# A two-layer hybrid encoder: the order of all five engines drawn on another machine model, and two dependent paths traced at the highest priority

## The chip, the cores and the metric

One Trainium2 chip, of which this program uses one core. The core has five engines that each run their own instruction stream in a fixed order: TensorE (PE, matmuls, with its weight loads shown apart as PEld), VectorE (DVE), ScalarE (ACT), GpSimd (POOL) and SyncE (SP, which here only issues DMAs). The metric is the device time of one launch in microseconds (us); lower is better.

## The reference

A sequence of 512 tokens with 1,024 channels in float32 passes two layers. Each layer normalises, projects once, runs four head groups side by side and projects back:

```python
for i in range(DEPTH):                                   # 2
    h = _rms_norm(x, pre_norm_w[i])                      # x: (1, 512, 1024)
    proj = jnp.einsum("bld,de->ble", h, w_in[i])
    (m_z, m_xbc, m_dt, r_u, r_g, d_q, d_k, d_v, d_g, g_q, g_k, g_v, g_g) = _split(proj, PROJ_SIZES)
    y_a = _mamba_mixer(m_z, m_xbc, m_dt, ...)            # conv, SSD scan in both directions, gated norm
    y_b = _rwkv_mixer(r_u, ...) * jax.nn.silu(r_g)       # delta-rule scan, 8 heads of 64, both directions
    y_c = _diff_mixer(d_q, d_k, d_v, ...) * jax.nn.silu(d_g)   # two softmax maps per head
    y_d = _gqa_mixer(g_q, g_k, g_v, ...) * jax.nn.silu(g_g)    # grouped-query attention
    mix = jnp.einsum("ble,ed->bld", jnp.concatenate([y_a, y_b, y_c, y_d], axis=-1), w_out[i])
    x = x + _rms_norm(mix, post_norm_w[i])
```

The two scans are recurrences. `_wkv7_scan` updates a 64x64 state per head and token with S = S*w + (S a) b + v k; `_ssd` does a scan in chunks of 128 tokens, in 2 groups of 4 heads, forwards and backwards. Everything else (the projections, the attention, the output product `mix`) has no order of its own beyond its inputs.

## The kernel before

**Matmuls and weights.** Products of the projections are made in three matmuls, high part by high part, high by low, low by high. A weight block of 128x512 comes in by a DMA of 256 KB that SP issues (`wf`), ACT makes its high part (`whi`, L144) and POOL its low part (`wlo`, L145), and PE uses the block in 24 matmuls of 256 columns (`pjt`, token-major) or 12 of 512 (`pjc`, channel-major). All of `mm` is L82.

**A layer.** After the first norm, `rwkv` runs: `prep(0)` prepares the first pair of heads, `products(0, 0)` makes the first `pa`, and then a loop over j in 0..3 (a pair of heads in both directions) has the solver and the chain. The solver is one dependent path: a transpose, 15 steps of substitution of two small DVE operations each (L560, L562), two transposes (L567, L568) into `DN` and `DT`, then products on PE, each copied out by ACT and DVE before the next: `pm`, three `ph`, `px`, `pu`, `pq`, `pw`, `pp`, `py`. The chain has 7 steps of `bk` on PE and one DVE operation (L663) each, and `yb`. In its last steps it also makes the next `pa` (`products(j + 1, 0)`), masked on DVE at L450, from which the next solver starts.

Beside the solver's steps the program traces two other kinds of work. `ahead` holds the preparation of the next pair, the transposes to tokens (`pb` among them) and the norm of the last pair. `fill` holds the filler: the projections of the two attentions (`pjt`), their scores `sc`, the transposed probabilities `ptp` and their products `ob`. The `F_` constants say how much filler, in modelled us, is traced after each step.

Then `ssd` runs: the path of the step size (`pjd`, `pcx`), `project(0)` (`pjc`, `pjt`, `pxt`, `pg`), and for each group g of two the same body: for 4 heads two `prow`, the differences on DVE (L811), exponentials on ACT (L814), scaling on DVE (L819, L820), `mt` (L823) and `yd`; then three steps of states (`stp`), four of outputs (`po`), and a norm. The filler beside group 0 is `project(1)`; beside group 1 it is `accumulate`, the output product `mix` with its transposes `ytr` (L1228) and its split of the weights and of y (L1234, L1241, L1242). The rest of `mix` follows the loop and ends the layer.

**What sets the order.** The tile framework takes the instructions in the order of tracing as their priority, gives them to a scheduler that plays them on a modelled machine, and writes each engine's stream in the order in which the model issued them. The streams are then fixed: on the chip an engine waits for the next instruction of its stream, whatever else may be ready behind it. So the place at which filler is traced is a wish, and the model decides.

Of the kernel before, what the change touches and what calls it, by code (L numbers as in the profile page):

```python
# [2 lines left out]

# [1 line left out]

# [26 lines left out]
F_S1 = 0.54  # L32
F_S2 = 0.67
F_S3 = 0.92
F_S4 = 1.0
# [40 lines left out]
def trunk(ctx: ExitStack, tc: tile.TileContext, x_in, win, wwd, wdt, wout, w2a, cols, rows, sscal, consts, out, dbg=None,  # L76
# [38 lines left out]

    x_dram = dpool.tile([L, D], F32, name="x_dram")
    y_dram = [dpool.tile([128, L], F32, name=f"y_dram{n}") for n in range(12)]

    def tap(name, ap, dst=None):
        if dbg is not None and name in dbg:  # L120
# [132 lines left out]
    def rwkv(i, lay, pw, ps, rp, fill):  # L253
# [271 lines left out]
        for j in range(4):  # L525
# [7 lines left out]
                ahead.gens.append(prep(j + 1))  # L533

            def step(n, us):
                ahead(n)
                fill(us)


            sv = rp.tile([128, 1536], F32, tag="sv", name="sv", bufs=1)  # L540
            As = sv[:, 0:1024].rearrange("p (t h s) -> p t h s", t=16, h=2)
# [108 lines left out]
            St = [Q[:, d, 0, :] for d in range(2)]  # L650
            for cc in range(1, 8):
                if cc == C_LAG:
                    ahead.finish()
                    if j < 3:
                        ahead.gens = [products(j + 1, 0)]
                Sn = [None, None]
                for d in range(2):
                    if cc < 7:
                        bk = ps.tile([128, 8, 64], F32, tag="g" if d else "ch", name=f"bk{d}")
                        for e in range(2):  # L660
                            mm(bk[half[e], 0, :], P[half[e], d, cc, :], St[d][half[e]], True, True)
                        Sn[d] = rp.tile([128, 64], F32, tag=f"S{d}", name=f"S{d}", bufs=2)
                        V.scalar_tensor_tensor(Sn[d], bk[:, 0, :], lamC[:, d, cc:cc + 1], Q[:, d, cc, :],  # L663
                                               op0=ALU.mult, op1=ALU.add)
                    for e in range(2):
                        mm(yb[half[e], rev(d, cc)], St[d][half[e]], R[half[e], d, cc, ::1 - 2 * d], False, True, True)
                St = Sn
                step(2, F_CH)
            ahead.finish()
            ys = rp.tile([128, L], F32, tag="tmp", name="ys", bufs=3)  # L670
            for b in range(2):
                sl = lambda t: t.rearrange("p (c b t) -> p c b t", c=4, b=2)[:, :, b, :]
                V.tensor_tensor(sl(ys), sl(yb), Y0[:, b], op=ALU.add)
        for _ in norm(3, ys):
            fill(F_GN / 4)
        fill.scale = 1.0
# [2 lines left out]
    def ssd(i, lay, ps, sp, op, yA, fill, more):  # L679
# [10 lines left out]
        for h, tag in enumerate(("whi", "wlo")):  # L690
# [2 lines left out]
            G.tensor_tensor(w[:, :, 1, :], wf[:, h], w.bitcast(F32)[:, :, 0, :], op=ALU.subtract)  # L693
            ws.append(w.rearrange("p k a n -> p k (a n)"))
        fill.settle()
        pd = ps.tile([128, L], F32, tag="pj", name="pjd")
        for k in range(8):
            mm(pd, ws[k // 4][:, k % 4, :], hT["hi"][:, k, :], k == 0, False)
# [39 lines left out]
            S.activation(colT[:, n], pcx, AF.Copy)  # L738
        exT = sp.tile([128, 4, 64], F32, tag="exT", name="exT")
        S.activation(exT, colT[:, 0], AF.Exp)  # L740

        gr = [{}, {}]

# [47 lines left out]
        for g in range(2):  # L791
            if g:
                fill.finish()
                fill.gens.extend(more)
            cv, zs, xs, bt, gT = (gr[g][n] for n in ("cv", "zs", "xs", "bt", "gT"))

            etot = sp.tile([128, 2, 4, 4], F32, tag="etot", name="etot")
# [2 lines left out]
            for h in range(4):  # L800
                ex = []
                for d in range(2):
                    ri = d * 8 + 4 * g + h
                    pr = ps.tile([128, L], F32, tag="g", name="prow")
                    mm(pr, selE[:, ri:ri + 1].to_broadcast([128, 128]), acs, True, True)
                    p4 = pr.rearrange("p (c t) -> p c t", c=4)
                    S.activation(etot[:, d, :, h:h + 1], p4[:, :, 127:128] if d == 0 else p4[:, :, 0:1], AF.Exp)
                    ar = sp.tile([128, 4, 128], F32, tag="ar", name="ar", bufs=2)
                    row = 32 * d + 4 * g + h
                    for ch in range(4):  # L810
                        V.scalar_tensor_tensor(ar[:, ch, :], p4[:, ch, :], colT[:, 0, ch, row:row + 1],  # L811
                                               mneg[:, d * 128:d * 128 + 128],
                                               op0=ALU.subtract, op1=ALU.min)
                    S.activation(ar, ar, AF.Exp)  # L814
                    ex.append(ar)
                    fill(F_S1)
                for ch in range(4):
                    row = 4 * g + h
                    V.tensor_scalar(ex[0][:, ch, :], ex[0][:, ch, :], colT[:, 1, ch, row:row + 1], None, op0=ALU.mult)  # L819
                    V.scalar_tensor_tensor(ex[1][:, ch, :], ex[1][:, ch, :], colT[:, 1, ch, row + 32:row + 33],  # L820
                                           ex[0][:, ch, :], op0=ALU.mult, op1=ALU.add)
                mt = sp.tile([128, 4, 128], F32, tag="mt", name="mt", bufs=2)
                V.tensor_tensor(mt, ex[1], gT, op=ALU.mult)  # L823
                fill(F_S2)
                if h % 2 == 0:
                    yd = ps.tile([128, 4, 2, 64], F32, tag="g", name="yd")
                for ch in range(4):
                    mm(yd[:, ch, h % 2, :], mt[:, ch, :], xs[:, ch, h * 64:h * 64 + 64], True, True)
                if h % 2 == 1:
                    S.activation(y[:, :, (h - 1) * 64:(h + 1) * 64], yd.rearrange("p c h v -> p c (h v)"), AF.Copy)  # L830

            H = [[None] * 4, [None] * 4]
            for step in range(3):
                stp = ps.tile([128, 2, 256], F32, tag="g", name="stp")
                for d in range(2):
                    ch = step if d == 0 else 3 - step
                    nx = ch + 1 if d == 0 else ch - 1
                    row = 32 * d + 4 * g
                    xd = sp.tile([128, 4, 64], F32, tag="xd", name="xd", bufs=2)
                    G.tensor_tensor(xd, xs[:, ch, :].rearrange("p (h v) -> p h v", h=4),  # L840
                                    colT[:, 2, ch, row:row + 4].unsqueeze(2).to_broadcast([128, 4, 64]), op=ALU.mult)
                    mm(stp[:, d, :], bt[:, ch, :], xd.rearrange("p h v -> p (h v)"), True, True)
                    hn = sp.tile([128, 256], F32, tag=f"H{d}{step}", name="H")
                    if step == 0:
                        V.tensor_copy(hn, stp[:, d, :])
                    else:
                        G.tensor_tensor(hn.rearrange("p (h v) -> p h v", h=4),
                                        H[d][ch].rearrange("p (h v) -> p h v", h=4),
                                        etot[:, d, ch, :].unsqueeze(2).to_broadcast([128, 4, 64]), op=ALU.mult)
                        V.tensor_tensor(hn, hn, stp[:, d, :], op=ALU.add)  # L850
                    H[d][nx] = hn
                fill(F_S3)
            for ch in range(4):
                po = ps.tile([128, 2, 256], F32, tag="g", name="po")
                ds = [d for d in range(2) if H[d][ch] is not None]
                for d in ds:
                    mm(po[:, d, :], cv[6 + g][:, ch * 128:ch * 128 + 128], H[d][ch], True, True)
                of = sp.tile([128, 2, 256], F32, tag="of", name="of", bufs=2)
                for d in ds:
                    row = 32 * d + 4 * g  # L860
                    V.tensor_tensor(of[:, d, :].rearrange("p (h v) -> p h v", h=4),
                                    po[:, d, :].rearrange("p (h v) -> p h v", h=4),
                                    exT[:, ch, row:row + 4].unsqueeze(2).to_broadcast([128, 4, 64]), op=ALU.mult)
                    G.tensor_tensor(y[:, ch, :], y[:, ch, :], of[:, d, :], op=ALU.add)
                fill(F_S4)
                sk = sp.tile([128, 256], F32, tag="sk", name="sk", bufs=2)
                G.tensor_tensor(sk.rearrange("p (h v) -> p h v", h=4), xs[:, ch, :].rearrange("p (h v) -> p h v", h=4),
                                rws[:, R_D + 4 * g:R_D + 4 * g + 4].unsqueeze(2).to_broadcast([128, 4, 64]), op=ALU.mult)
                V.scalar_tensor_tensor(y[:, ch, :], sk, 0.5, y[:, ch, :], op0=ALU.mult, op1=ALU.add)
# [5 lines left out]
                jk = sp.tile([128, 256], F32, tag="sk", name="jk", bufs=2)  # L875
                S.activation(jk, y[:, ch, :], AF.Square, accum_out=ss[:, ch:ch + 1])
            r = rstd(sp, ss, 4, 1.0 / 256, EPS)
            fill(F_S5)
            yA[g] = zs
            for ch in range(4):  # L880
                V.scalar_tensor_tensor(yA[g][:, ch, :], y[:, ch, :], r[:, ch:ch + 1],  # L881
                                       rws[:, R_SSM + g * 256:R_SSM + g * 256 + 256], op0=ALU.mult, op1=ALU.mult)
            tap("ya", yA[g], lambda a: a[:, g * 256:g * 256 + 256].rearrange("(c p) v -> p c v", p=128))


    def softmax_rows(sc, ap):
# [565 lines left out]
```

## Time and profile before

| | us |
|---|---|
| runs | 1826.45, 1837.58, 1839.16 (median 1837.58) |
| the profiled execution | 1827.76, of which the span is 1826.0 |
| granted TensorE clock, mean of the span | 0.93 |
| PE busy | 1596.3, 87% of the span |
| DVE busy | 1088.5, 60% |
| ACT busy | 826.5, 45% |
| POOL busy | 695.9, 38% |

The page gives the busy time of each engine over the span, which for PE says how long some matmul was in flight and not how fast it went. The granted clock says which share of full speed the chip allowed to TensorE. The stretches below are cut at events of the program in layer 1: the first `pm` of each j (143.5, 294, 452.5, 591 us), the end of the last chain (676), the first `prow` of the SSD's group 0 (734) and the end of its last `po` and start of group 1 (about 795), the last `po` of group 1 (839) and the end of `mix` (901). Layer 2 repeats them from about 943 us on.

### The profile page before, as it was taken

The numbers are of one execution on the slowest core, as the hardware profiler recorded it, in microseconds if no ns is written. First come the engines' busy times: TensorE is split into PE (matmuls) and PEld (weight loads), VectorE is DVE, ScalarE is ACT, GpSimd is POOL, SyncE is SP. The second block draws the span as 40 slices with busy tenths as digits, with TensorE's granted clock in tenths as the row PEclk, the third lists the DMA queues.
The fourth block names the chain that finished last, engine by engine and source line by source line (L and its number), as shares of the span: only waits on it lengthen the run. The fifth ranks groups of instructions, "written<-read, shape, count | busy, mean of one in ns | idle before, by whom it ended". The sixth has DMA issues, their size and how long they took to land. (4 is left out here: it accounts for less than half of the span.)

```text
span 1826.0 us, 36868 instructions
## 1 busy us (share of the span) xinstructions
PE 1596.3 (87%) x15232; PEld 1321.8 (72%) x15232; DVE 1088.5 (60%) x2130; ACT 826.5 (45%) x1602; POOL 695.9 (38%) x708
## 2 busy tenths in 40 slices
PE   6888889879899898988887998898788989989888
PEld 6677767757788776766775787677567777768666
DVE  3577576575555437885245865755755554288852
ACT  4645336417345335543346453454272453454431
POOL 4543234242424234543455422343333332245333
PEclk9889989989999998999998899899898999989899
DMA  4110001011101014122321100111110110131223
GB/s 148 64 50 32 29 33 59 14 67 35 42 19 62 28 53 138 59 94 81 127 99 54 53 20 29 34 59 36 44 42 31 36 58 22 54 130 53 87 86 116
DMA packets 57512, 108.50 MB, mean 59 GB/s; under 512 B 6784, under 2 KB 8704, under 8 KB 57344
## 3 DMA queue, kind: packets, MB, share of 16 engines
q1 hardware_dynamic: 57344, 106.15, 17.4%
q8 instruction: 119, 1.95, 0.4%
q14 instruction: 49, 0.40, 0.1%
HBM read 95.64 MB, written 10.49 MB: 58 GB/s over the span
## 5 line engine op out<-in xcount | busy, mean ns | idle before, releaser
L145 POOL TENSOR_TENSOR wlo<-wf,whi 128x512 fp32r<-128x512 f32 x228 | 319.6, 1408 | 423.8 <-ACT whi L144 391.3
L82 PE MATMUL pjt<-whi,hhi 128*128 128x256 f32 x960 | 291.3, 303 | 3.7 <-ACT raw L270 1.7
L82 PE MATMUL pjt<-wlo,hhi 128*128 128x256 f32 x960 | 284.5, 297 | 0.8 <-POOL wlo L145 0.8
L82 PE MATMUL pjt<-whi,hlo 128*128 128x256 f32 x960 | 285.2, 297 | 0.0
L144 ACT ACTIVATE whi<-wf 128x512 fp32r<-128x512 f32 x228 | 142.1, 627 | 226.3 <-PE pjt L82 122.6
L82 PEld LDWEIGHTS pjt<-whi,hhi 128*128 128x128 f32 x960 | 191.8, 200 | 15.6 <-issue 7.3
L82 PEld LDWEIGHTS pjt<-whi,hlo 128*128 128x128 f32 x960 | 191.9, 200 | 6.1 <-issue 5.0
L82 PEld LDWEIGHTS pjt<-wlo,hhi 128*128 128x128 f32 x960 | 191.2, 199 | 5.2 <-issue 3.3
L82 PE MATMUL pjc<-hhi,whi 128*128 128x512 f32 x384 | 160.0, 417 | 16.9 <-ACT craw L751 10.7
L82 PE MATMUL pjc<-hhi,wlo 128*128 128x512 f32 x384 | 157.4, 410 | 3.5 <-POOL wlo L145 3.5
L82 PE MATMUL pjc<-hlo,whi 128*128 128x512 f32 x384 | 156.5, 407 | 0.0
L82 PE MATMUL mix<-whi,ylo 128*128 128x512 f32 x256 | 105.8, 413 | 5.5 <-DVE ylo L1234 5.5
L892 ACT ACTIVATE p<-sc,nm 128x512 f32<-128x512 f32 x96 | 65.6, 685 | 89.0 <-DVE nm L889 81.8
L82 PE MATMUL mix<-wlo,yhi 128*128 128x512 f32 x256 | 103.7, 405 | 0.0
L82 PEld LDWEIGHTS pjc<-hhi,whi 128*128 128x128 f32 x384 | 75.0, 195 | 39.5 <-ACT craw L751 12.4
L82 PE MATMUL mix<-whi,yhi 128*128 128x512 f32 x256 | 99.8, 412 | 4.0 <-ACT yhi L1233 4.0
L889 DVE TENSOR_REDUCE nm<-sc 128x1 f32<-128x512 f32 x96 | 64.5, 689 | 63.2 <-PE sc L82 63.1
L82 PE MATMUL pa<-AR,BK 64*64 64x128 f32 x1024 | 66.3, 341 | 37.7 <-DVE AT L450 37.5
L82 PEld LDWEIGHTS pjc<-hhi,wlo 128*128 128x128 f32 x384 | 75.2, 196 | 23.3 <-POOL wlo L145 5.6
L82 PE MATMUL sc<-qT,qT 64*128 64x512 f32 (+1 forms) x256 | 86.4, 478 | 3.8 <-ACT y L1050 1.8
L82 PEld LDWEIGHTS pa<-AR,BK 64*64 64x64 f32 x1024 | 52.8, 171 | 48.7 <-DVE AT L450 42.4
L82 PEld LDWEIGHTS pjc<-hlo,whi 128*128 128x128 f32 x384 | 75.6, 197 | 15.0 <-issue 0.7
(360 smaller groups left out, 3645.4 us busy)
## 6 DMA issues: line engine op xcount, KB each, us to landing
wf<-in_win_dram SPq DMA_DIRECT2D x224, 256.0 KB, 3.0
wf<-in_wout_dram SPq DMA_DIRECT2D x64, 256.0 KB, 2.7
y<-y_dram SPq DMA_DIRECT2D x24, 256.0 KB, 3.4
xt<-in_x_dram SPq DMA_DIRECT2D x8, 512.0 KB, 4.2
y_dram<-y SPq DMA_DIRECT2D x16, 256.0 KB, 3.3
y_dram<-rs SPq DMA_DIRECT2D x8, 256.0 KB, 2.8
x_dram<-t SPq DMA_DIRECT2D x8, 256.0 KB, 2.1
xt<-x_dram SPq DMA_DIRECT2D x4, 512.0 KB, 4.0
```

The costliest lines, as they stand in the source:

```text
L82: PE.matmul(o, lhsT, rhs, start=start, stop=stop, skip_group_check=skip)
L144: S.activation(hi, wf, AF.Copy)
L145: G.tensor_tensor(lo, wf, hi.bitcast(F32), op=ALU.subtract)
L889: V.tensor_reduce(nm, sc, axis=AX, op=ALU.max, negate=True)
L892: S.activation(p, sc, AF.Exp, bias=nm, accum_out=sm)
```

## The change

The tile context gets `schedule_with_timeline_sim=True`: the order is drawn by playing the instructions on another model of the machine, the timeline machine, with the same priorities as far as the program gives them. And two paths are traced inside `tc.high_priority()`, which puts them ahead of everything else that is ready: the RWKV's solver and chain of each j, and the SSD's step-size path and its body per group. The calls of `ahead` and `fill` within are wrapped in `usual()`, which leaves the high priority for their length. `prep(0)`, `project`, the attention and `accumulate` stay at the usual priority. The instructions and their number are the same; their lines move down by 9 to 23.

```diff
+    urgent = ExitStack()
+
+    @contextmanager
+    def usual():
+
+        urgent.close()
+        yield
+        urgent.enter_context(tc.high_priority())
...
             def step(n, us):
-                ahead(n)
-                fill(us)
-
+                with usual():
+                    ahead(n)
+                    fill(us)
+
+            urgent.enter_context(tc.high_priority())
...
                 if cc == C_LAG:
-                    ahead.finish()
+                    with usual():
+                        ahead.finish()
                     if j < 3:
                         ahead.gens = [products(j + 1, 0)]
...
                 V.tensor_tensor(sl(ys), sl(yb), Y0[:, b], op=ALU.add)
+            urgent.close()
...
         fill.settle()
+        urgent.enter_context(tc.high_priority())
         pd = ps.tile([128, L], F32, tag="pj", name="pjd")
...
         S.activation(exT, colT[:, 0], AF.Exp)
+        urgent.close()
...
             if g:
                 fill.finish()
                 fill.gens.extend(more)
+            urgent.enter_context(tc.high_priority())
...
                     ex.append(ar)
-                    fill(F_S1)
+                    with usual():
+                        fill(F_S1)
...
             tap("ya", yA[g], lambda a: a[:, g * 256:g * 256 + 256].rearrange("(c p) v -> p c v", p=128))
+            urgent.close()
...
-    with tile.TileContext(nc) as tc:
+    with tile.TileContext(nc, schedule_with_timeline_sim=True) as tc:
```

The calls `fill(F_S2)` to `fill(F_S5)` are wrapped in the same way as `fill(F_S1)`.

**PE's stream in layer 1, at the first `pa` of the first pair of heads, before:**

```order
L82 MATMUL pa<-AR,BK 64x128 x7
L82 MATMUL pjt<-wlo,hhi 128x256
L82 MATMUL pa<-AR,BK 64x128 x8
L82 MATMUL pjt<-whi,hhi 128x256
L82 MATMUL pjt<-whi,hlo 128x256
L82 MATMUL pjt<-wlo,hhi 128x256
L82 MATMUL pjt<-whi,hhi 128x256
L82 MATMUL pa<-AR,BK 64x128 x16
```

The same place with the change:

```order
L82 MATMUL pjc<-hlo,whi 128x512
L82 MATMUL pjc<-hhi,wlo 128x512
L82 MATMUL sc<-qT_1312,qT_1303 128x512
L82 MATMUL sc<-qT_1312,qT_1304 128x512
L82 MATMUL sc<-qT_1313,qT_1303 128x512
L82 MATMUL pa<-AR,BK 64x128 x16
L82 MATMUL pjt<-whi,hhi 128x256
L82 MATMUL pjt<-whi,hlo 128x256
L82 MATMUL pjt<-wlo,hhi 128x256
```

Before, the sixteen `pa` of a direction stand among single matmuls of an attention projection (`pjt`); with the change they stand in one piece behind a whole weight block of an RWKV projection (`pjc`) and three score matmuls (`sc`, with the buffer numbers of their tiles). Counted over the stream, 609 matmuls stand ahead of the first `pm` before and 825 with the change: 163 `pjt`, 24 `sc`, 12 `ptp`, 12 `ob` and 4 `pqt` of the filler more, and one `yb`. Between that `pm` and the last `bk` of layer 1 stand 163 `pjt`, 26 `sc`, 28 `ptp`, 32 `ob` and 4 `pqt` less, and 24 `pjc` and 16 `pjd` more.

**PE's stream in layer 1, in the SSD's second group, before:**

```order
L82 MATMUL mix<-wlo,yhi 128x512
L82 MATMUL mix<-whi,yhi 128x512
L82 MATMUL mix<-whi,ylo 128x512
L82 MATMUL yd<-xs,mt 128x64 x4
L82 MATMUL prow<-acs,cr 128x512
L82 MATMUL mix<-wlo,yhi 128x512
L82 MATMUL mix<-whi,yhi 128x512
L82 MATMUL mix<-whi,ylo 128x512
L82 MATMUL mix<-wlo,yhi 128x512
L1228 MATMUL ytr<-cst,y 128x128 x7
L82 MATMUL prow<-acs,cr 128x512
L1228 MATMUL ytr<-cst,y 128x128
```

The same place with the change, from the end of `project(1)` on:

```order
L793 MATMUL pxt<-cst,cv 128x128 x12
L82 MATMUL pg<-cv 128x128 x4
L82 MATMUL prow<-acs,cr 128x512 x2
L1251 MATMUL ytr<-cst,zs 128x128 x8
L82 MATMUL yd<-xs,mt 128x64 x4
L82 MATMUL prow<-acs,cr 128x512 x3
L82 MATMUL yd<-xs,mt 128x64 x4
L82 MATMUL prow<-acs,cr 128x512
L82 MATMUL yd<-xs,mt 128x64 x4
L82 MATMUL prow<-acs,cr 128x512 x2
L82 MATMUL stp<-xd,bt 128x256 x2
L82 MATMUL yd<-xs,mt 128x64 x4
```

Before, the output product (`mix`) stands between the group's own matmuls, 104 of them from the group's first `prow` to its last `po`, with 28 `ytr`; with the change none stands there, and 8 `ytr`. The 144 `mix` of this kind now stand in group 0 (none stood there before), with 96 `pjt` in place of 58, 76 `pjc` in place of 93 and 32 `ytr`; between the groups 17 `mix` and 38 `pjt` are gone. From the last `po` to the end of the layer there are 240 `mix` in place of 263 and 8 `ytr` in place of 20. Layer 2 is moved in the same way.

## Rows read from the trace of the kernel before

**Rows 1.** The page, busy time (share of the span) and instructions of each engine, whole run.

```profile
PE 1596.3 (87%) x15232; PEld 1321.8 (72%) x15232; DVE 1088.5 (60%) x2130; ACT 826.5 (45%) x1602; POOL 695.9 (38%) x708
```

**Rows 2.** Busy us (x instructions) by stretch of layer 1; PEclk: granted TensorE clock.

```profile
40.00:143.50 103.50, 89.81 (x497) 70.31 (x495) 70.72 (x100) 56.65 (x92) 54.15 (x49) 0.88 0.19 63
143.50:294.00 150.50, 134.44 (x1569) 111.53 (x1568) 97.26 (x189) 72.68 (x135) 48.91 (x46) 0.93 0.10 35
294.00:452.50 158.50, 134.34 (x1594) 111.73 (x1593) 97.08 (x183) 74.97 (x146) 52.94 (x52) 0.92 0.12 40
452.50:591.00 138.50, 124.81 (x1569) 108.72 (x1569) 76.57 (x178) 62.60 (x140) 51.53 (x49) 0.91 0.11 36
591.00:676.00 85.00, 78.94 (x1192) 66.45 (x1190) 35.63 (x93) 28.47 (x67) 20.95 (x26) 0.98 0.13 41
676.00:734.00 58.00, 48.81 (x264) 38.87 (x259) 39.59 (x50) 33.17 (x54) 30.17 (x35) 0.91 0.39 128
734.00:795.00 61.00, 52.36 (x284) 43.40 (x283) 52.30 (x114) 26.90 (x57) 33.65 (x39) 0.97 0.18 58
795.00:839.00 44.00, 41.53 (x207) 32.88 (x208) 34.44 (x96) 16.89 (x35) 14.52 (x17) 1.00 0.29 90
839.00:901.00 62.00, 58.52 (x251) 46.72 (x250) 19.77 (x30) 22.79 (x47) 22.91 (x21) 0.94 0.34 115
```

**Rows 3.** Timeline of DVE: start us, us long, instruction; end of the first substitution.

```profile
129.61 1.98 DVE L568 STREAM_TRANSPOSE DT<-sv 128x1024 f32<-128x1024 f32 x1
```

**Rows 4.** Timeline of PE: start us, us long, instruction [idle before <-releaser].

```profile
93.99 0.28 PE L82 MATMUL pjt<-whi,hhi 128*128 128x256 f32 x1
94.10 0.28 PE L82 MATMUL pjt<-whi,hlo 128*128 128x256 f32 x1
97.62 0.80 PE L82 MATMUL p<-bh,cr 128*128 128x512 f32 x1 [3.24 <-ACT bh L292]
...
104.60 0.41 PE L82 MATMUL pjt<-wlo,hhi 128*128 128x256 f32 x1
104.81 0.41 PE L82 MATMUL pjt<-whi,hhi 128*128 128x256 f32 x1
...
143.56 0.45 PE L82 MATMUL pm<-DN,AT 64*64 64x64 f32 x8
```

**Rows 5.** PE's waits over the whole run: total us, times, longest.

```profile
PE pa L82 <- DVE AT L450: 37.5, 13, 8.5
PE pb L458 <- DVE Mp L576: 14.2, 6, 3.8
```

**Rows 6.** One more stretch, columns as in Rows 2.

```profile
97.50:111.10 13.60, 13.48 (x107) 10.60 (x109) 6.49 (x8) 2.86 (x6) 6.63 (x6) 0.50 0.16 57
```

**Rows 7.** The page, groups by line: busy us, mean ns | idle before, releaser.

```profile
L145 POOL TENSOR_TENSOR wlo<-wf,whi 128x512 fp32r<-128x512 f32 x228 | 319.6, 1408 | 423.8 <-ACT whi L144 391.3
...
L144 ACT ACTIVATE whi<-wf 128x512 fp32r<-128x512 f32 x228 | 142.1, 627 | 226.3 <-PE pjt L82 122.6
```

**Rows 8.** Timeline of PE in the first solver, columns as in Rows 4.

```profile
191.73 0.60 PE L914 MATMUL ptp<-cst,p 128*128 128x128 f32 x4
...
193.08 1.16 PE L82 MATMUL ob<-v,ptS 128*128 128x128 f32 x8
```

**Rows 9.** Timeline of PE in the second SSD group, columns as in Rows 4.

```profile
796.25 0.39 PE L82 MATMUL mix<-wlo,yhi 128*128 128x512 f32 x1
796.48 0.39 PE L82 MATMUL mix<-whi,yhi 128*128 128x512 f32 x1
...
826.21 1.03 PE L1228 MATMUL ytr<-cst,y 128*128 128x128 f32 x8
...
828.82 1.10 PE L82 MATMUL yd<-xs,mt 128*128 128x64 f32 x8 [0.56 <-DVE mt L823]
```

**Rows 10.** DVE's work by line in 795 to 839 us: busy us, mean ns.

```profile
L1234 DVE TENSOR_TENSOR ylo<-ytr,yhi 128x512 fp32r<-128x512 f32 x7 | 4.7, 680 | 0.0
...
L1242 DVE TENSOR_TENSOR wlo<-wf,whi 128x512 fp32r<-128x512 f32 x4 | 2.7, 687 | 0.0
```

More of the change, by code (lines that the diff above doesn't have):

```diff
@@ L1 @@
 import math
-from contextlib import ExitStack
+from contextlib import ExitStack, contextmanager
 import numpy as np
@@ L668, in rwkv @@
                 step(2, F_CH)
-            ahead.finish()
+            with usual():
+                ahead.finish()
             ys = rp.tile([128, L], F32, tag="tmp", name="ys", bufs=3)
@@ L815, in ssd @@
                     ex.append(ar)
-                    fill(F_S1)
+                    with usual():
+                        fill(F_S1)
                 for ch in range(4):
@@ L823, in ssd @@
                 V.tensor_tensor(mt, ex[1], gT, op=ALU.mult)
-                fill(F_S2)
+                with usual():
+                    fill(F_S2)
                 if h % 2 == 0:
@@ L851, in ssd @@
                     H[d][nx] = hn
-                fill(F_S3)
+                with usual():
+                    fill(F_S3)
             for ch in range(4):
@@ L864, in ssd @@
                     G.tensor_tensor(y[:, ch, :], y[:, ch, :], of[:, d, :], op=ALU.add)
-                fill(F_S4)
+                with usual():
+                    fill(F_S4)
                 sk = sp.tile([128, 256], F32, tag="sk", name="sk", bufs=2)
@@ L877, in ssd @@
             r = rstd(sp, ss, 4, 1.0 / 256, EPS)
-            fill(F_S5)
+            with usual():
+                fill(F_S5)
             yA[g] = zs
```

## The prediction

> **What bounds the kernel now.** I began with the busy times of the page: PE is in use for 87% of the span, no other engine for more than 60% [rows 1]. The reader is to see there that PE is the only candidate, and that the number does not say whether it runs at its peak. The table by stretch says that it does not [rows 2]. The four stretches of the RWKV loop (143.5 to 676 us) last 150.5 + 158.5 + 138.5 + 85 = 532.5 us, with PE busy 134.4 + 134.3 + 124.8 + 78.9 = 472.5: 60.0 us idle. Their granted clocks of 0.93, 0.92, 0.91 and 0.98 lose at most 10.5 + 12.7 + 12.5 + 1.7 = 37.4 more. So 97 us of 532.5 are loss, the rest is work that stays whatever the order. The SSD's second group is the opposite: 795 to 839 us at clock 1.00 with 41.5 of 44 busy. Before the first `pm` (40 to 143.5) 13.7 us are idle and the clock of 0.88 loses 12.4.
>
> Is the loss in the loop the length of the dependent path, or work in a poor order? The timeline of DVE and PE shows the second at the first `pm`: its operands are complete when the transpose into `DT` ends at 129.61 + 1.98 = 131.6 us [rows 3], and `pm` starts at 143.56 [rows 4], 12 us later, since filler stands ahead of it in PE's stream. PE's waits show the first elsewhere: it waits 37.5 us in all for the masked `AT` after the `pa` at the end of the chain, and 14.2 for `Mp` [rows 5]: 51.7 us, 26 per layer, in which PE's stream holds nothing in between.
>
> Each idle stretch has a second price. After 3.24 us of idle before `p` at 97.62 the `pjt` follow each other every 0.21 us (104.60, 104.81) in place of 0.11 (93.99, 94.10) [rows 4], and the 13.6 us from 97.5 run at a granted clock of 0.50 [rows 6], the lower level of 1.2 GHz.
>
> **The change, stretch by stretch (one layer).** No instruction goes or comes; PE work is moved, at full-clock spacings: `pjt` 0.12 [rows 4], `mix`, `pjc` and, as a bound, `sc` 0.23 (796.25 to 796.48), `ytr` 1.03/8 = 0.13 [rows 9], `ptp` 0.60/4 = 0.15, `ob` 1.16/8 per half, so 0.29 each [rows 8].
>
> *Before the first `pm`.* The order puts 216 matmuls more there: 163 x 0.12 + 24 x 0.23 + 12 x 0.29 + 12 x 0.15 + 4 x 0.15 = 31 us. They find 13.7 idle and 12.4 of lost clock, so the stretch grows by 5 to 31. I take **+10**, near the lower end, because this work is the kind whose shortage makes the loss, and the first solver no longer waits for filler. The 163 `pjt` are 7 weight blocks: 7 x 1.41 on POOL and 7 x 0.63 on ACT [rows 7], where POOL has 54.2 and ACT 56.7 of 103.5 busy [rows 2]: hidden. Without that cover, had POOL been full, they would cost 10 us.
>
> *The RWKV loop.* Of filler, 163 `pjt`, 26 `sc`, 28 `ptp`, 32 `ob` and 4 `pqt` leave; 24 `pjc` and 16 `pjd` come: 39.6 - 9.2 = **-30**. If the dependent path set every length, this would save nothing; 12 us of slack at the first `pm` speak against it. The second part is what priority does to the 97 us of loss: the solver's DVE and PE operations stand close together and no longer behind filler. It can be nothing (the waits for `AT` lie between dependent operations of the path itself, where a priority cannot help unless something else fills them) or all 97. I take **-20**, the nearest row being the 26 us per layer of waits for `AT` and `Mp`, and not all of them are to go. The Trainium skill (Perfetto Trace Analysis, "Identifying the Most-Contended Engine") calls PE's busy share an unreliable measure of headroom and reads the weight loads in its place. By it the four stretches (PEld 111.5 + 111.7 + 108.7 + 66.5 = 398.4) have 134 us of room, not 97; a fifth of that is 27, and the total would come out at about 1766.
>
> *End of the chain to the first `prow` (676 to 734).* 20 `ob`, 16 `ptp` and 2 `sc` come, 16 `pjd` and 7 `pjc` leave: +3 us into 9.2 idle: **0**; uncovered it is +3.
>
> *SSD, group 0 and up to group 1.* 144 `mix` come and 17 leave, 32 `ytr` come, 17 `pjc` leave, the `pjt` even out: 127 x 0.23 + 32 x 0.13 - 17 x 0.23 = +29. Busy 52.4 [rows 2] becomes 81 in a stretch of 61; with 2 us of idle left it is 83: **+22**, at most +29 (all idle stays).
>
> *Group 1.* 104 `mix` and 20 `ytr` leave, 26 us, so 41.5 - 26 = 15 of PE is left. But PE does not set the length any more: DVE has 34.4 busy there [rows 2], of which the `ylo` and `wlo` of the output product, 4.7 + 2.7, can leave [rows 10]. So 27 is the floor and 44 the ceiling; the group is a chain over PE, DVE, ACT and POOL, and its first `yd` already follow DVE's `mt` (0.56 at 828.82) [rows 9]. I take 40: **-4**. This is the one place where the change uncovers something: 26 us of PE work that ran beside DVE for nothing now runs elsewhere, at its own price.
>
> *Rest of the layer.* 23 `mix` and 12 `ytr` less: -7. Against it, `mix` begins behind 25 us of thin PE work, and I allow half of the 6.8 us that the stretch at clock 0.50 lost [rows 6], +3: **-4**. The Trainium skill speaks against this part of the change (TensorE: Matmul & The Clock Gate, "HAM oscillation — how this bites in real kernels"): matmuls that run dry while they wait for other work fall back to half speed each time. By it the whole 6.8 is due at each such tail, and the total would be 8 us higher, 1788.
>
> Sum per layer: 10 - 30 - 20 + 0 + 22 - 4 - 4 = -26; layer 2 repeats the pattern: -52. The profiled execution took 1827.8 us (span 1826.0), so 1776 against it. The median of the three runs, 1837.6, is 9.8 above that execution; I add half of it: **1780 us**, 3% below the median.
>
> **Rivals.**
> *A. Denser than I think.* The loop loses 60 of its 97 us per layer in place of 20, and group 1 takes 35 in place of 40: 45 us less per layer, about 1690. For it: `pm` started 12 us late for no reason of its own. Against it: the waits for `AT` are in the path itself. Chance 0.12.
> *B. No difference.* The loop gives 26 per layer and not 50 (filler now runs out before the last chain, where 96 `pjt` are gone), which the first stretch and the SSD eat: 10 - 26 + 22 - 4 - 4 = -2, about 1825 to 1838. Chance 0.19. That the order would not really change is excluded by the two orders.
> *C. Slower: the bare second group of the SSD.* Its place is 795 to 839 us. There PE was the bound at clock 1.00 and DVE ran beneath it; bare, the group's chain takes its 44 us still, while its 26 us of PE work is paid for in group 0, which is full. Then the SSD costs 22 to 29 per layer, 25 in the middle, with no gain behind it; with the +10 of the first stretch that is 35, and the rival decides if the path sets the loop's length and the loop shortens by less than 35. With the loop at -10 it is +25 per layer: about 1827.8 + 50 + 5 = 1883. For it: the 51.7 us of waits inside the path, and that a drawn order which is wrong about one duration makes PE stand at the head of its stream with work ready behind it. Against it: the slack at the first `pm`. Chance 0.17.
>
> **How the numbers follow.** The forecast has 0.52, A 0.12, B 0.19, C 0.17. The forecast's own spread comes from the first stretch (+5 to +31), the loop's second part (0 to -40 here) and group 1 (35 to 44), about 20 per layer to either side: 1740 to 1820. The range leaves out most of A below and most of C above: **1705 to 1858**. About 1% is what a measurement of this kernel can tell from no change, 18 us. Faster by more (below 1819): 0.52 + 0.12 and a little of B, 0.66; within: 0.17; slower (above 1856): 0.17.
>
> **What would show it.** In the table by stretch of the changed kernel: the first `pm` comes 5 to 15 us later than 143.5; the four stretches up to the last chain sum to 475 to 490 in place of 532.5, with clocks above 0.95 if the loss goes; `pm` follows `DT` within 2 or 3 us; group 0 with the stretch between takes about 83 at clock 1.00; group 1 takes 35 to 44 with PE busy about 15, DVE about 27 and no `mix`, and its waits name DVE's `mt`. If the loop's sum stays above 510, the path sets it and I am wrong towards C; if group 1 exceeds 44, the bare chain is dearer than PE's work was; if the waits for `AT` and `Mp` stay at 51.7 us and the time falls all the same, the gain is the work moved and not the priority.

## The result: slower by 1%

Four runs of the changed kernel took 1849.8 to 1854.5 us, median 1852.44; the kernel before took 1834.01 beside them. The ratio is 1.0099, with a 95% interval of 1.0073 to 1.0125. The forecast was 1780 us, with a range of 1705 to 1858: the time is inside the range and on the wrong side of no change.

The table by stretch of the kernel after, cut at the same events of layer 1 as [rows 2] but for its ends (busy us of PE, PEld, DVE, ACT, POOL; granted clock; DMA share, GB/s). The first row begins at 36 us and not at 40. The last goes to the end of `mix`, which in the kernel before comes at 918.4 us and not at the 901 that is given for it above:

```profile
36.00:159.70 123.70, 115.36 (x746) 94.20 (x745) 78.58 (x123) 72.10 (x128) 68.22 (x58) 0.99 0.20 66
159.70:296.90 137.20, 123.19 (x1477) 102.15 (x1476) 88.47 (x174) 61.48 (x116) 50.04 (x47) 0.94 0.10 34
296.90:450.80 153.90, 135.75 (x1563) 113.39 (x1562) 93.89 (x178) 74.35 (x147) 55.49 (x50) 0.93 0.12 41
450.80:584.90 134.10, 120.74 (x1563) 106.03 (x1561) 93.00 (x192) 62.38 (x139) 50.75 (x50) 0.96 0.11 37
584.90:654.10 69.20, 65.22 (x1073) 56.10 (x1072) 31.82 (x70) 21.45 (x43) 18.57 (x21) 0.95 0.13 44
654.10:723.90 69.80, 56.03 (x295) 45.69 (x291) 42.56 (x56) 36.51 (x66) 25.66 (x34) 0.85 0.31 102
723.90:806.50 82.60, 80.05 (x438) 67.68 (x436) 60.57 (x125) 37.08 (x68) 32.86 (x37) 1.00 0.31 97
806.50:855.50 49.00, 26.14 (x75) 17.45 (x73) 28.45 (x89) 9.56 (x27) 11.73 (x18) 0.55 0.00 1
855.50:923.90 68.40, 58.00 (x248) 46.78 (x248) 22.02 (x37) 23.43 (x50) 25.38 (x23) 0.93 0.34 111
```

The reader is to see two rows. Up to 654 us the change has gained 22 us (the last `bk` ended at 676). Then the SSD's second group (806.5 to 855.5) stands there with PE busy for 26 of 49 us at a clock of 0.55 and no DMA at all. Set beside the old stretches, with the exact events (in us, before to after):

| stretch | forecast | layer 1 | layer 2 |
|---|---|---|---|
| layer's start to the first `pm` | +10 | 143.6 to 159.7, +16 | 130.6 to 152.6, +22 |
| first `pm` to the last `bk` | -50 | 532.5 to 494.4, -38 | 531.9 to 495.7, -36 |
| to the first `prow` | 0 | 57.9 to 69.8, +12 | 59.7 to 67.4, +8 |
| SSD group 0 and up to group 1 | +22 | 62.0 to 82.6, +21 | 62.8 to 82.4, +20 |
| SSD group 1 | -4 | 42.7 to 49.0, +6 | 43.7 to 48.7, +5 |
| to the end of `mix` | -4 | 79.7 to 68.4, -11 | 71.0 to 70.1, -1 |

The columns sum to +6 and +17 before rounding, 23 us in all; the spans differ by 22. So the RWKV part (the first two rows) gained 22 and 14, and the rest lost 28 and 31.

PE's waits over the whole run, of those that the forecast named in [rows 5] and of those that came in their place (total us, times, longest), then the wait for `DN` in the kernel before:

```profile
PE mix L82 <- ACT yhi L1256: 21.1, 2, 10.9
PE ph L82 <- DVE DN L600: 16.8, 12, 3.8
...
PE px L82 <- DVE DN L600: 9.4, 2, 5.9
...
PE pv L467 <- DVE AT L459: 3.7, 3, 1.3
...
PE pa L82 <- DVE AT L459: 3.2, 3, 1.3
PE pk L467 <- DVE AT L459: 3.1, 3, 1.2
...
PE pb L467 <- DVE Mp L587: 0.5, 1, 0.5
```

```profile
PE ph L82 <- DVE DN L589: 2.2, 2, 1.1
```

The two waits of [rows 5] fell from 51.7 us to 3.7; 6.8 more for the same `AT` now stand at the transposes `pv` and `pk`. In their place PE waits 26.2 us for `DN` inside the solver (2.2 us in the kernel before) and, behind the bare second group, 21.1 for the next `yhi`.

### The profile page after: what moved, and what is told of

It is laid out like the page before. It is cut to its first block, busy times and chain, and to the rows that moved or that the text cites. A ratio compares the mean times of both kernels' runs of the same rounds, so it can differ in the third digit from the quotient of the medians.

```text
span 1848.0 us, 36885 instructions
## 1 busy us (share of the span) xinstructions
PE 1606.6 (87%) x15232; PEld 1343.8 (73%) x15232; DVE 1108.7 (60%) x2130; ACT 821.9 (44%) x1602; POOL 699.6 (38%) x708
## 5 line engine op out<-in xcount | busy, mean ns | idle before, releaser
L154 POOL TENSOR_TENSOR wlo<-wf,whi 128x512 fp32r<-128x512 f32 x228 | 318.3, 1402 | 410.5 <-ACT whi L153 361.6
L82 PE MATMUL pjt<-whi,hhi 128*128 128x256 f32 x960 | 287.0, 300 | 8.6 <-ACT gqk L1025 5.4
L82 PE MATMUL mix<-whi,yhi 128*128 128x512 f32 x256 | 93.2, 408 | 21.4 <-ACT yhi L1256 21.1
L915 ACT ACTIVATE p<-sc,nm 128x512 f32<-128x512 f32 x96 | 65.6, 683 | 95.6 <-DVE nm L912 67.4
L82 PE MATMUL sc<-qT,qT 64*128 64x512 f32 (+1 forms) x256 | 90.4, 489 | 11.9 <-ACT p L915 8.4
L82 PE MATMUL mix<-wlo,yhi 128*128 128x512 f32 x256 | 99.7, 396 | 0.0
L1265 POOL TENSOR_TENSOR wlo<-wf,whi 128x512 fp32r<-128x512 f32 x32 | 42.6, 1333 | 121.9 <-ACT whi L1264 108.3
L82 PE MATMUL ob<-v,ptS 128*128 128x128 f32 x512 | 76.6, 292 | 10.9 <-ACT ptS L939 10.9
```

Source lines behind the costliest of these rows:

```text
L82: PE.matmul(o, lhsT, rhs, start=start, stop=stop, skip_group_check=skip)
L154: G.tensor_tensor(lo, wf, hi.bitcast(F32), op=ALU.subtract)
L915: S.activation(p, sc, AF.Exp, bias=nm, accum_out=sm)
L1265: (V if kt % 2 else G).tensor_tensor(lo, wf, hi.bitcast(F32), op=ALU.subtract)
```

## The experiments

My first theory was **cover**: the output product is the only work that can stand beside group 1, the new machine had spent it beside group 0, and holding it back would return the 31 us or so per layer that stand open there. Its rivals are written out with each run. Each ratio is to runs of the kernel before on the same chip. Their medians lay between 1832.0 and 1839.3 us on the chips used, so a difference of a few us between two of the experiments says nothing.

**Holding the output product back (e1, e2).** A zero that is made from group 1's `gT` becomes the bias of one weight split, so that `mix` can't start earlier; nothing is left out of the computation.

```diff
+                V.tensor_scalar(hold, gr[1]["gT"][:, 0, 0:1], 0.0, None, op0=ALU.mult)
...
+            if (kt, hf) == (4, 0):          # e2: (7, 0)
+                S.activation(hi, wf, AF.Identity, bias=hold)
+            else:
+                S.activation(hi, wf, AF.Copy)
```

> The changed kernel, in which the output product beside the SSD (mix, its blocks 4 to 15) can start only when project(1) is done: its first weight block gets a zero bias taken from gT of group 1. 144 mix per layer move from group 0 to group 1, nothing else moves. Theory 'cover': the changed kernel loses 31 us per layer where group 1 stands bare (49 us with 26 of PE busy, half of that at half clock). Then group 1 takes 43 to 50 us with PE busy about 42 at clock 1.0, group 0 with the stretch up to group 1 falls from 82.6 to 50 to 62 (41 us of PE work left), and the time falls by 40 to 65 us to 1790 to 1812. Rival 'path': group 0 is as long as it is because project(1)'s own path through DVE is late, whatever PE does; then group 0 stays near 80 and the time stays within 10 us of 1852.

> As before, but only blocks 7 to 15 of the output product wait for group 1: 36 mix stay beside group 0, 108 go to group 1. Cover: group 0 has 49 us of PE work, group 1 34; both stretches are as long as with blocks 4 to 15 held or a few us shorter, so 1785 to 1812. If group 0 is bound by PE's work alone, it is 8 us longer per layer than with all blocks held, and group 1 not shorter: 16 us more. Path: within 10 us of 1852.

e1 took 1836.7 us (before: 1835.4; ratio 1.0016, 0.9997 to 1.0034), e2 1837.7. That is 16 below the changed kernel, but outside the bands of the theory and of the rival alike. The two groups in e1, layer 1, columns as above:

```profile
725.30:793.60 68.30, 57.47 (x294) 46.62 (x292) 52.12 (x118) 27.28 (x52) 22.92 (x29) 0.83 0.18 55
793.60:857.30 63.70, 54.18 (x218) 41.92 (x217) 36.37 (x96) 19.10 (x43) 21.85 (x25) 0.84 0.22 67
```

68.3 + 63.7 = 132.0 us, where the changed kernel has 82.6 + 49.0 = 131.6 and the kernel before 104.7. (e2: 132.3.) The cover moved from one group to the other and the sum stayed. The 16 us come from the RWKV loop of layer 2, 478.2 us in place of 495.7, which was drawn otherwise. **Cover alone falls as the cause.** The rival does not hold either: its group 0 was to stay near 80. But with 144 `mix` less (33 us at the forecast's spacing) group 0 is still 6 us longer than in the kernel before, so PE's work is not all that sets its length.

What makes a covered group 63.7 us long shows in PE's timeline of e1 and in DVE's:

```profile
809.91 0.48 PE L82 MATMUL prow<-acs,cr 128*128 128x512 f32 x1
...
816.18 0.40 PE L82 MATMUL prow<-acs,cr 128*128 128x512 f32 x1
...
822.38 0.40 PE L82 MATMUL prow<-acs,cr 128*128 128x512 f32 x1
```

```profile
810.64 1.13 DVE L829 SCALAR_TENSOR_TENSOR ar<-prow,colT,mneg 128x128 f32<-128x128 f32 x4 [3.22 <-ACT etot L825]
...
816.83 1.13 DVE L829 SCALAR_TENSOR_TENSOR ar<-prow,colT,mneg 128x128 f32<-128x128 f32 x4 [3.49 <-ACT etot L825]
```

One `prow` every 6.2 us, with `mix` in between and PE never idle; DVE stands idle for over 3 us before each. In the bare group of the changed kernel they follow each other more closely, though the clock is at its lower level there:

```profile
817.51 0.77 PE L82 MATMUL prow<-acs,cr 128*128 128x512 f32 x1
819.81 0.77 PE L82 MATMUL prow<-acs,cr 128*128 128x512 f32 x1 [1.52 <-DVE ar L828]
822.47 0.77 PE L82 MATMUL prow<-acs,cr 128*128 128x512 f32 x1 [1.90 <-DVE ar L828]
```

2.3 and 2.7 us. In the kernel before, where `mix` stands beside group 1 too, it is 2.0 and 2.9:

```profile
803.50 0.48 PE L82 MATMUL prow<-acs,cr 128*128 128x512 f32 x1
...
805.50 0.47 PE L82 MATMUL prow<-acs,cr 128*128 128x512 f32 x1
...
808.42 0.40 PE L82 MATMUL prow<-acs,cr 128*128 128x512 f32 x1
```

So the path can step in 2.5 us, beside `mix` or bare, and in the stream drawn for e1 it is let through every 6.

**The machine or the priorities (e3, e4).** e3 is the kernel before with `schedule_with_timeline_sim=True` alone; e4 is the changed kernel without it.

> The kernel before with the order drawn by the timeline machine and no priorities. Its stream in the SSD is that of the changed kernel (144 mix in group 0, none in group 1). Cover: the loss in the SSD, 25 us per layer, is there in full; the RWKV loop has 9 to 10 us per layer more filler before the last bk of the chain, and is longer by that and by what priority saves (a guess of 5 to 10): 1855 to 1890. Rival 'priorities harm' (the urgent path pushes filler to places where it does not cover): faster than the changed kernel, 1820 to 1845.

> The changed kernel with the default machine drawing the order: priorities alone. Its SSD is that of the kernel before (108 mix beside group 1), but beside the last solver and chain of each layer only 67 pjt are left as filler, and 35 us of attention work stands between the last bk and the first prow. Cover: the SSD costs nothing, the bare last chain of the loop shortens by 10 to 20 us where 32 us of work leave, the stretch behind it grows by 30 to 40: 1840 to 1880. Priorities harm: slower than the changed kernel, over 1870. If priorities help and the flag harms: 1790 to 1825.

e3: 1847.6 us (1.0084, 1.0054 to 1.0115), with the two groups at 130.9 us. e4: 1838.1 (1.0024, 1.0000 to 1.0048), with the groups at 107.7. The SSD's loss belongs to the machine, not to the priorities. e3 lies 7 us below its band, 3 above the rival's, and 5 below the changed kernel, which the intervals of the two ratios do not tell apart: the priorities were no gain as the kernel stands. e4 lies 2 us below its first band and in none of the others. In e4 the last solver and chain of layer 1 ran nearly without filler in 41.4 us (84.9 before), and the stretch behind it took 111.5 (57.9 before):

```profile
582.20:623.60 41.40, 39.30 (x939) 35.16 (x939) 16.02 (x35) 10.22 (x23) 5.07 (x4) 1.00 0.10 31
623.60:735.10 111.50, 95.01 (x581) 80.08 (x578) 63.26 (x109) 56.25 (x110) 48.47 (x59) 0.89 0.30 90
```

**Transplanting the order (e5, e6, e7, e9).** The instructions have the same names in both kernels. A table lists the SSD's own instructions per engine, in the order of the other kernel, and an edge of issue order (no wait) ties each to the one ahead of it:

```diff
+    for t in tables:
+        prev = None
+        for n in t:
...
+            if prev is not None:
+                tc.add_manual_dep(insts[n], prev, info, reason="graft")   # info: NoSync
+            prev = n
```

The theory is now **drawn order of the SSD**, the rival **context**.

> The changed kernel with edges of pure issue order (no waits) that make every engine issue the SSD's own instructions (from pjd to the end of the output product, both layers) in the order of the kernel before; the RWKV part keeps its changed order. Theory 'drawn order of the SSD': what the change loses is that on the timeline machine the SSD's path stands behind too much filler in PE's stream (a prow every 6 us in the covered parts, where the bare path needs 2.5), so the two groups take 132 us in place of 105 wherever the output product stands. Then the groups take 100 to 110 per layer again, and the time falls by 2 x 25 us and up to 2 x 5 more: 1785 to 1805, which beats both kernels. Rival 'context': the RWKV's new order leaves the SSD other work and other buffers, and the SSD is slow for that, whatever its own order: 1835 to 1855.

> The reverse: the kernel before with the SSD's instructions issued in the changed kernel's order on every engine, and its own order in the RWKV part. Drawn order of the SSD: groups 128 to 135 us, so 1835 + 2 x 25 to 2 x 35: 1880 to 1905. Context: within 10 us of 1835.

> As e5, but PE alone issues the SSD in the order of the kernel before; DVE, ACT, POOL and SP keep what the timeline machine draws around it. If the loss is in PE's stream alone (prow behind filler): the same as e5 within 6 us. If the orders on DVE and ACT (convolutions of project(1) against the path's own steps) carry a part of it: between e5 and the changed kernel, 10 us or more above e5.

> The changed kernel with the SSD's instructions on DVE, ACT, POOL and SP in the order of the kernel before, and PE's left to the timeline machine (the reverse of e7). If DVE and ACT carry the larger part (convolutions of project(1) in one piece ahead of the path's steps): within 15 us of e5, 1793 to 1808. If PE's stream carries it: 1815 to 1840, and e7 and e9 each give a part of the 60 us between e5 and the changed kernel.

e5 took **1792.75 us** (ratio 0.9781, 0.9746 to 0.9815), e6 1897.5 (1.0343, 1.0302 to 1.0385): both as the first theory said. The groups of layer 1, e5 and then e6:

```profile
723.50:786.40 62.90, 54.23 (x294) 45.31 (x292) 53.61 (x118) 26.89 (x57) 34.77 (x39) 0.93 0.19 57
786.40:829.90 43.50, 40.99 (x199) 32.39 (x199) 33.24 (x91) 16.89 (x35) 13.12 (x16) 0.98 0.29 91
```

```profile
743.90:827.10 83.20, 79.89 (x436) 67.69 (x435) 59.05 (x126) 37.12 (x68) 33.65 (x37) 1.00 0.32 96
827.10:875.40 48.30, 25.98 (x75) 17.49 (x73) 27.76 (x87) 9.57 (x27) 11.03 (x18) 0.54 0.00 1
```

106.4 and 131.5 us: each order carries its length into the other kernel. The order of the kernel before also puts `mix` back beside group 1; since e1 moved `mix` without gain in the groups, what is shown is the order as a whole, and not which part of it counts. The changed RWKV order alone is worth -44 us, the changed SSD order alone +60, and -44 + 60 = +16 is about the +18 of both.

e7, with PE alone in the old order: 1835.0 (1.0004), groups 117.2 us. e9, with the four other engines in the old order and PE drawn: 1892.9 (1.0308), groups 143.1. e7's second expectation holds: it is 42 us above e5, and 17 below the changed kernel. e9 misses both bands, it is 40 us worse than the changed kernel. One wait of PE grows where the two orders meet; here it is in the kernel before, the changed kernel, e7 and e9:

```profile
PE yd L82 <- DVE mt L823: 4.9, 10, 0.7
```

```profile
PE yd L82 <- DVE mt L841: 12.5, 4, 4.1
```

```profile
PE yd L82 <- DVE mt L841: 22.2, 16, 4.9
```

```profile
PE yd L82 <- DVE mt L841: 37.0, 8, 6.4
```

In e5 it is 5.3 us. The orders of single engines do not add up: PE's old order alone returns 17 of the 60 us, that of the other four alone costs 40, and all five together return the 60. The wait does not account for all of this, since e7 has more of it than the changed kernel and is faster.

**The priorities again, beside a good SSD order (e8).** e3 plus e5's table.

> The timeline machine without any priorities, with the SSD issued on every engine in the order of the kernel before. It asks what the high priority of the solver and chain is worth beside the new machine. Theory 'the machine does it': the priorities are worth under 8 us in all, since the loop's stretches took 499 and 490 us without them and 494 and 496 with them: 1785 to 1801. Rival 'the priority does it': they carry the loop's gain, and without them the time is above 1805.

1807.7 us (0.9838, 0.9794 to 0.9881): 15 above e5, so "the machine does it" misses and the rival's band holds, though the two ratios' intervals overlap. Of the difference nothing is in layer 1 (first `pm` to last `bk` 498.0 in e8, 498.9 in e5); it is in layer 2, whose loop was drawn otherwise (511.4 and 498.6). By e3 the priorities cost up to 5 us, and here they give up to 15. I don't take either for the worth of a priority.

**What holds the solver (e10, e11, e12).** The forecast wanted `pm` 2 or 3 us behind `DT`. In the kernel after:

```profile
140.53 2.18 DVE L579 STREAM_TRANSPOSE DT<-sv 128x1024 f32<-128x1024 f32 x1
```

```profile
159.26 0.49 PE L82 MATMUL p<-bh,cr 128*128 128x512 f32 x1 [1.01 <-ACT bh L301]
159.69 1.15 PE L82 MATMUL pm<-DN,AT 64*64 64x64 f32 x32
```

It is 17 us behind, more than the 12 before [rows 3, 4], and right behind a `p` of `prep(1)`, as at 143.56 in the kernel before. Both take their PSUM banks (the buffers that matmuls write) from tag `g`, which has two, and `prep(1)` is traced ahead of `pm`. Over all eight j the distance sums to 174 us before, 132 with the change, and 171 in e4.

```diff
-            pm = banks(G2, [128, 8, 64], "pm")
+            pm = banks(("ch", "yb"), [128, 8, 64], "pm")
```

> The changed kernel with the two PSUM banks of pm taken from the tags ch and yb, which are free at that time, in place of two of tag g, which pm shares with the products of prep(j + 1) traced ahead of it. Theory 'banks': pm stands 17 us behind its operands because a bank of tag g comes to it only after prep's own product, whatever its priority. Then pm starts within 5 us of the end of the transpose into DT (17 us before), the first pm at 144 to 150 us in place of 159.7. For the time: the solver is ahead by some 10 us per j, but PE's work stays; 10 to 25 us less, 1827 to 1842. Rival 'filler': the place of pm in PE's stream is the timeline machine's choice of filler; then pm stays 12 us or more behind DT, and the time within 6 us of 1852.

> The same beside the SSD's order of the kernel before (e5 plus the other banks for pm). Banks: 10 to 25 us below e5, 1768 to 1783. Filler: within 6 us of 1793.

> The kernel before with the banks of pm taken from ch and yb, and nothing of the change. Theory 'banks need the order': the other banks only allow pm to go earlier; without the new machine and the priority its place stays the default machine's choice of filler, and only 25 PE instructions fewer stand ahead of the first pm: pm at 138 to 143 us in layer 1, time within 8 us of the kernel before. Rival 'banks alone': the shared banks are what held pm here too, pm follows DT within 5 us and the time falls by 15 to 30 us to 1805 to 1820.

e10: 1826.3 us (0.9961, 0.9942 to 0.9980), 26 below the changed kernel. Its `DN`, `DT` and `pm`:

```profile
137.44 2.36 DVE L578 STREAM_TRANSPOSE DN<-sv 128x1024 f32<-128x1024 f32 x1
139.49 2.12 DVE L579 STREAM_TRANSPOSE DT<-sv 128x1024 f32<-128x1024 f32 x1
```

```profile
141.04 2.08 PE L82 MATMUL pm<-DN,AT 64*64 64x64 f32 x64
```

`pm` needs only `DN` and now starts before `DT` is done, in all eight j. The sum of the distances is -11 us in place of 132. The rival "filler" is out; the time is 1 us under the theory's band. The gain is where the solver is: from the layer's start to the last `bk` e10 takes 645.7 and 631.3 us in the two layers, the changed kernel 654.1 and 648.3, and the SSD's groups stay at 131.3. e11, the same beside e5's table, is the fastest version: **1780.97 us** (0.9717, 0.9672 to 0.9762), 12 below e5; its four runs (1777.1 to 1787.5) and those of e5 (1791.1 to 1798.4) do not overlap. e12, the banks in the kernel before alone: 1829.5 (0.9960, 0.9936 to 0.9984), 7 below it. Its first `DT` and `pm`:

```profile
129.99 2.04 DVE L568 STREAM_TRANSPOSE DT<-sv 128x1024 f32<-128x1024 f32 x1
```

```profile
137.58 1.09 PE L82 MATMUL pm<-DN,AT 64*64 64x64 f32 x30
```

The first distance of each layer falls from 12 us to 5.5; the other six stay at 17 to 40. The banks allow it, the new order uses it. Whether the priorities or the timeline machine do so no run tells: the other banks were not tried with one of the two alone.

## Why the prediction was wrong

*What came out.* PE as the only candidate, and 97 us of loss in the loop, held. The differences from the forecast, summed over both layers, are 18 us in the first stretch, 26 in the loop, 20 to the first `prow`, 19 in group 1, and -4 each in group 0 and the rest: 75 us, spread over four stretches, and only the loop's is large enough to turn the sign by itself. That the time is inside the range is owed to the range's upper end, which lies above no change.

*The first stretch.* +10 forecast, +16 and +22 measured: inside the 5 to 31 that the step allowed, but the choice "near the lower end" was wrong. In layer 1 the clock is 0.99 in place of 0.88, so the added work did its part there; 8.3 of the 13.7 us of idle time stayed.

*The step that failed: the priority's cure in the loop (-50 forecast, -38 and -36 measured).* I read 12 us of slack before `pm`, "since filler stands ahead of it in PE's stream", as a poor order that a priority cures, and `pm` was to follow `DT` within 2 or 3 us. In the changed kernel it comes 10 to 21 us behind, 132 in all. What holds it there is a bank of PSUM that, by the program's text, comes to it only after the products of `prep` that are traced before it: e4, with the priority alone, has the slack in full, and e10 removes it with one line and takes back 26 us. The bank is not the whole of it, since in the kernel before the other banks alone leave most of the slack (e12). The operands were read wrongly too: `pm` needs `DN` alone, so the first slack was 13.8 us. The same sentence carried the weight against rivals B and C.

*The loop's two terms.* By the forecast's measure (idle plus what the granted clock loses) layer 1's loop after has 49.5 + 27.8 = 77 us: 20 less, as forecast, half of it idle time and half clock. That this size came out is in part luck: the waits for `AT` and `Mp` fell, but more than half as much waiting for `DN` and `AT` came in their place, and most of the slack before `pm` is still there. What fell short is the other term: 30 us of PE work left, and gave back only 18. Why, the runs don't show.

*The second step that failed: group 1 of the SSD.* Group 0 came out at the forecast 83 us, with PE busy for 80 at clock 1.00 as forecast. Group 1 I set at 40, between a floor of 27 and the 44 of before; it took 49. Cut at the third and the last `prow` of the group, after and then before:

```profile
806.50:817.50 11.00, 4.54 (x21) 3.38 (x20) 8.90 (x25) 3.59 (x13) 3.66 (x5) 0.70 0.00 0
817.50:836.00 18.50, 7.32 (x24) 4.90 (x23) 10.86 (x38) 4.03 (x11) 0.00 (x0) 0.50 0.00 0
836.00:855.50 19.50, 14.28 (x33) 9.16 (x33) 8.69 (x26) 1.95 (x4) 8.07 (x13) 0.51 0.00 1
```

```profile
795.90:803.50 7.60, 7.60 (x40) 6.28 (x39) 5.67 (x22) 3.15 (x7) 2.04 (x2) 1.00 0.18 54
803.50:822.60 19.10, 18.11 (x95) 14.30 (x95) 16.77 (x45) 9.11 (x20) 2.58 (x3) 1.00 0.46 144
822.60:838.60 16.00, 14.57 (x69) 11.09 (x68) 11.10 (x28) 4.62 (x9) 8.61 (x12) 1.00 0.16 49
```

The middle takes as long bare at half clock as covered at full clock. The head is 3.4 us longer: on DVE two steps of group 0's norm, done before group 1 begins in the kernel before, now stand ahead of its first `mt`:

```profile
807.56 1.52 DVE L893 SCALAR_TENSOR_TENSOR y<-y,zs 128x1024 f32<-128x1024 f32 x1
...
813.40 1.66 DVE L903 SCALAR_TENSOR_TENSOR zs<-y,rstdr,srow 128x256 f32<-128x256 f32 x4
814.99 0.68 DVE L841 TENSOR_TENSOR mt<-ar,gT 128x512 f32<-128x512 f32 x1
```

The tail is 3.5 us longer, at a clock of 0.51 in place of 1.00, where PE's own work is dense:

```profile
850.14 5.36 PE L82 MATMUL po<-H,cv 128*128 128x256 f32 x12 [0.58 <-DVE H L869]
```

The last twelve `po` took 2.99 before. So the ceiling "44" left out the lower clock and the place of the norm. The Trainium skill's rule (TensorE: Matmul & The Clock Gate, "HAM oscillation — how this bites in real kernels") was weighed for the stretch behind the group only; the 0.55 of this stretch agrees with it inside the group too. In the time of the kernel the SSD's order counts for more than its miss against the forecast: most of its price was in the forecast (+22 - 4 per layer), and e5 gets back some 60 us by undoing it.

*To the first `prow`.* 0 forecast, +12 and +8 measured, at clock 0.85 and 0.90 in place of 0.91 and 0.89; PE's idle time there rose by 5 us in each layer. e5 has +6 and 0, e6 +7 and +6: a part goes with either order. Why this term failed is not settled.

*The rivals.* C priced the SSD at +22 to +29 per layer, and the two groups cost 27 and 25. Its condition was that the loop gave back less than 35; it gave 38 and 36, and the stretches around it took back 28 and 30. So the result lies between B and C.

## What to carry to other kernels

A priority decides among instructions that are ready. In this kernel it did not move `pm` ahead of the tiles that share its banks and are traced before it. Where an urgent product stands late, look first which other tiles share its banks and are traced ahead of it. A fixed order is one thing over all engines: judge it by stretch, and when one stretch is worse, transplant that stretch's old order on every engine at once; here moving the cover within the new order left the two groups together as long as they were, and one engine's old order alone returned 17 of 60 us.

## What the runs showed that I had not expected

A path that is covered by filler can be slower than the bare one at half clock: a `prow` every 6.2 us with PE always busy, every 2.3 to 2.7 us with PE at a granted clock of 0.50. It is the drawn order and not the cover: in the kernel before the covered path steps as fast as the bare one. And two orders that are each consistent, mixed by engine, gave 1893 us, more than either of them (1793 and 1852). Why the timeline machine lets the SSD's path through so seldom was not tried and stays open.
